# Block steps of a feed-forward layer spread over longer chains, with one weight sum on GpSimd

## The chip, the cores and the metric

The kernel runs on one core of a Trainium2 chip. The metric is the device time of one execution, in microseconds (us); the kernel before was timed three times. All times of single instructions below come from one profiled execution.

The engines go by short names: PE is TensorE's matmul, PEld its weight load, DVE VectorE, ACT ScalarE, POOL GpSimd, SP SyncE, which here only issues transfers. POOL and ACT issue transfers too. Each engine takes its instructions in order, and waits on semaphores for the others.

## The reference, cut to what matters

One layer of an encoder on 512 tokens of width 1024: a gated linear attention branch (GLA) and a forgetting attention branch (FoX), merged by gates and an output projection, and then the feed-forward part, which the change is about:

```python
def causal_dwconv(u, w, bias):
    S = u.shape[1]
    up = jnp.pad(u, ((0, 0), (CONV_W - 1, 0), (0, 0)))
    out = bias
    for j in range(CONV_W):
        out = out + w[j] * up[:, j:j + S]
    return out
...
    y = jax.nn.sigmoid(g_gla + gate_b[0]) * (o_gla @ w_gla_branch) \
        + jax.nn.sigmoid(g_fox + gate_b[1]) * (o_fox @ w_fox_branch)
    x = x + y @ w_out

    a, val = jnp.split(rmsnorm(x, norm_ffn_g) @ w_up, 2, axis=-1)
    a = causal_dwconv(a, conv_w, conv_b)
    return x + (jax.nn.gelu(a) * val) @ w_down
```

Everything is float32. `w_up` is 1024 x 5632, `w_down` 2816 x 1024; a last RMSNorm follows.

## The kernel before, in words

**Products.** Each float32 operand is split into two parts, high and low, of a format that TensorE takes in one pass; `mm3` makes one product of three matmuls (high x high, high x low, low x high: lines 200 to 202). An activation operand is split once. A weight comes in pieces of 128 x 1024 (512 KB): `load_raw` (L136) issues its transfer from SP into a tile `raw` or `rawx`, two of each, and `split_next` (L162) makes `wh` with a ScalarE copy (L180) and `wl` with a VectorE subtraction (L181). Three `wh`/`wl` pairs go round. `piece()` (L191) hands out pieces in the order of the list `recipes` and splits three ahead.

**Stages in order of time.** To about 130 us the GLA stage (first projections, the chunked recurrence); to about 250 us attention; to about 320 us the branch projections and gates; to about 380 us the output projection, in which each of eight tiles also adds into the sum of squares for the next norm; then two plain feature tiles of `w_up`, the up stage from about 404 us, the down stage from about 620 us, and the end.

**The up stage.** The product with `w_up` is done in blocks, seven products instead of eight for each 2 x 2 block product (Winograd's variant of Strassen's scheme). The remaining 20 feature tiles form ten groups `g`, each with seven *steps* p1 to p7. A step is 24 matmuls of 256 columns (`up_product`, L998). Its weight operand is a piece or a running sum of pieces: p5 needs u12 + u11, p6 adds u22 to p5's, p4 adds u21 to p6's, p7 adds u12 to p3's. Before, every such addition is a transfer that adds into the tile in SBUF, issued from GpSimd's queue (L149 for p5, L184 for the others). An add can only be issued once the piece before it has been split, and the next piece only be split once the add has landed. So p5-p6-p4 and p3-p7 are *chains*, and the order of the steps sets how much time each link has. `SLOT` (L55) gives each step a place in a cycle of seven; the steps of all groups are sorted by it.

The results meet in PSUM: p1 and p2 in a bank `x`, p5 and p3 in `z`, p6, p7 and p4 in `y`. After p1 and after p5 the bank is copied to SBUF (`joint`, L1027, ScalarE). After p6 VectorE adds p1's copy to `y` into a new tile (L1030), ScalarE writes that back over `y` in PSUM (L1031), and VectorE makes the first half of the convolution's input `ap` from it and `z` (L925 within `minus_sum`). After p7 comes the second half, the convolution and gelu (L966, L970, L975); after p4 the activations (L1046) and their block sums. The tile framework plans the order of each engine's queue from the program order and its own estimates, so instructions of neighbouring steps mix.

**Ahead of the up stage.** `rms_of_sum` (L287) makes the norm's factor: matmuls with ones (L291), a short VectorE chain, a matmul that broadcasts (L296), a copy into `rb`. Products of the first plain tile stand before and between. VectorE then scales all of `xs` (L928) and, with ScalarE, makes the seven activation operands (`split_x`, L920).

**The down stage** has the same seven products, with operands made of activations and weights; the four weight blocks that are sums (`wsum`) are made in DRAM by eight transfers of 2816 KB, four copies and four adds, each issued from GpSimd (L189) behind the split of the piece named in `SUM_AT` (L57), after a tiny copy `tick` (L187) that waits for that split. Pieces of the down stage are loaded four ahead, into `raw` and `rawx`. The product `p` = 0 uses a11, which is complete after half of the up stage's groups.

Of the kernel before, what the change touches and what calls it, by code (L numbers as in the profile page):

```python
# [54 lines left out]
SLOT = {1: -3, 5: -1, 2: 1, 3: 2, 6: 3, 7: 5, 4: 7}  # L55

SUM_AT = (24, 27, 30, 33, 38, 42, 46, 50)  # L57
# [7 lines left out]
def hybrid_kernel(ctx: ExitStack, tc, xT, wp, wu, wd, wf, pp, aw2, qkg, fing, out):  # L65
# [24 lines left out]
    def pax():  # L90
        return bank("ax")
# [19 lines left out]
    recipes = [((wf[n],), None, WF, None) for n in range(KD)] + [((w,), None, 1024, "raw") for w in wp_pieces(wp)]  # L111
    steps = sorted((7 * g + at, g, p) for g in range(NSS) for p, at in SLOT.items())
    steps = [(g, p) for _, g, p in steps]
    at_step = {}
    for g, p in steps:
# [7 lines left out]
    ND = len(recipes)  # L123
    for b in down_blocks:
        for i in range(NPB):
            m = min(1024, KB * 512 - i * 1024)
            place = "rawx" if (len(recipes) - ND) % (NRAW + NRAWX) >= NRAW else "raw"
            recipes.append(((b[:, i * 1024 : i * 1024 + m],), None, m, place))
    NP = len(recipes)
    follows = {r[1]: n for n, r in enumerate(recipes) if r[1] is not None}  # L130
# [5 lines left out]
    def load_raw(n):  # L136
        new, before, m, place = recipes[n]
        if before is not None:
            raws[n] = raws[before]
            return  # L140
        if n < KD:
            raws[n] = slabs[n]
        elif place == "raw":
            raws[n] = wpool.tile([P, 1024], F32, tag="raw", name="raw", bufs=NRAW)
        else:
            raws[n] = rawx_pool[0].tile([P, 1024], F32, tag="rawx", name="rawx", bufs=NRAWX)
        nc.sync.dma_start(raws[n][:, :m], new[0])
        for w in new[1:]:
            nc.gpsimd.dma_start(raws[n][:, :m], w, accum_op=ALU.add)  # L149

    def load_ahead(n):

        for i in range(n, min(NP, n + 6)):
            new, before, _, place = recipes[i]
            if place == "rawx":
                ahead = 6 if rawx_pool and i < ND else NRAW + NRAWX if rawx_pool else 0
            else:
# [1127 lines left out]
```

## Time and profile before

| | us |
|---|---|
| median of 3 runs (lowest, highest) | 740.61 (738.9, 741.93) |
| the profiled execution | 743.6 |
| its span, first to last instruction | 741.8 |
| PE busy | 714.4 (96%) |
| DVE busy | 518.7 (70%) |
| ACT busy | 407.4 (55%) |
| POOL busy | 166.9 (23%) |

In the rows of the profile `out<-in` names tiles; the two numbers of a timeline row are its start and its length in us; what stands in square brackets is idle time of that engine ahead of the instruction and what ended it. In a row of waits stand the engine and line that waited, what it waited for, and total us, times and longest. A window's row gives, for a stretch of time, its length, busy time and number of instructions of PE, PEld, DVE, ACT and POOL, the granted clock of TensorE, the busy share of the transfer engines and GB/s. A row of transfers ends with KB each and the median us from issue to landing. Matmuls are pipelined, so PE's busy share is not its share of the peak.

### The profile page before, as it was taken

To read this page: it belongs to the slowest core of one execution; us is meant where nothing else is said; L and a number is where in the kernel's file an instruction comes from. 1 tells how busy PE (TensorE), PEld (TensorE's weight loads), DVE (VectorE), ACT (ScalarE), POOL (GpSimd) and SP (SyncE) were. 2 spreads that over 40 slices of the span, in tenths; PEclk is the share of its full clock that TensorE was granted. 3 is DMA by queue.
4 is the path that set the end of the run, shared out by engine and by line. 5 is a ranking of instruction groups with operands and counts; after the bars stand their busy time and mean duration, and the time that the engine had idled before them with its cause. 6 is when DMAs were issued, how large, how long until landed. Compare 5 with 4: busy or idle time off the path is not lost.

```text
span 741.8 us, 11096 instructions
## 1 busy us (share of the span) xinstructions
PE 714.4 (96%) x4186; PEld 620.2 (84%) x4186; DVE 518.7 (70%) x787; ACT 407.4 (55%) x648; POOL 166.9 (23%) x190
## 2 busy tenths in 40 slices
PE   8999999999999999999999889899899998999996
PEld 6887788887888788877778789899899997888875
DVE  7875588577766654455439988577678876987876
ACT  7483333688778533225535556555455654655654
POOL 7133235224410321122320211011111101000113
PEclk9999999999999999999999999999999999999999
DMA  8052211787691987994564588788887888566653
GB/s 304 30 173 101 84 63 63 285 235 222 191 250 70 239 210 197 233 232 155 175 184 106 107 213 196 197 207 190 199 192 187 203 193 289 159 211 193 190 173 128
DMA packets 44117, 134.05 MB, mean 181 GB/s; under 512 B 4488, under 2 KB 11800, under 8 KB 43936
## 3 DMA queue, kind: packets, MB, share of 16 engines
q1 hardware_dynamic: 27552, 81.38, 33.8%
q0 software_dynamic: 10272, 46.66, 29.9%
q10 hardware_dynamic: 6240, 5.31, 2.2%
q8 instruction: 33, 0.54, 0.3%
q14 instruction: 20, 0.16, 0.1%
HBM read 129.12 MB, written 27.28 MB: 211 GB/s over the span
## 4 chain that ended last, share of the span: by engine, by line
PE 61%; DMA 17%; DVE 9%; issue 6%; ACT 4%; POOL 1%; SPq 0%; ACTq 0%; POOLq 0%; DVEq 0%
PE ps_mm L200 15%; PE ps_mm L201 14%; PE ps_mm L202 14%; DMA rawx<-in_wu_dram 7%; DMA raw<-in_wu_dram 6%; DVE wl L181 4%; PE ps_ax L201 4%; PE ps_ax L200 4%; PE ps_ax L202 4%; ACT wh L180 3%; DMA raw<-in_wp_dram 2%; DVE t L970 1%; DMA cb<-nct 1%; DMA rawx<-wsum 1%; PE ps_pt L737 1%
## 5 line engine op out<-in xcount | busy, mean ns | idle before, releaser
L180 ACT CAST wh<-raw 128x1024 fp32r<-128x1024 f32 x116 | 120.4, 1040 | 198.6 <-PE ps_mm L201 50.3
L181 DVE TENSOR_TENSOR wl<-raw,wh 128x1024 fp32r<-128x1024 f32 x116 | 153.2, 1323 | 74.8 <-ACT wh L180 73.8
L200 PE MATMUL ps_mm<-xh,wh 128*128 128x512 f32 (+1 forms) x288 | 102.0, 355 | 4.1 <-ACT ps_mm L1031 3.3
L202 PE MATMUL ps_mm<-xh,wl 128*128 128x512 f32 (+1 forms) x288 | 100.8, 351 | 0.0
L201 PE MATMUL ps_mm<-xl,wh 128*128 128x512 f32 (+1 forms) x288 | 100.8, 351 | 0.0
L200 PEld LDWEIGHTS ps_mm<-xh,wh 128*128 128x128 f32 x288 | 55.8, 194 | 11.4 <-ACT ps_mm L1031 4.1
L181 DVE TENSOR_TENSOR wl<-rawx,wh 128x1024 fp32r<-128x1024 f32 (+1 forms) x48 | 57.8, 1208 | 7.3 <-ACT wh L180 7.0
L202 PEld LDWEIGHTS ps_mm<-xh,wl 128*128 128x128 f32 x288 | 55.8, 194 | 7.4 <-DVE wl L177 0.4
L201 PEld LDWEIGHTS ps_mm<-xl,wh 128*128 128x128 f32 x288 | 56.0, 194 | 5.9
L180 ACT CAST wh<-rawx 128x1024 fp32r<-128x1024 f32 (+1 forms) x48 | 49.1, 1023 | 16.5 <-DMA rawx<-in_wu_dram 9.1
L200 PE MATMUL ps_mm<-wh,xh 128*128 128x512 f32 x140 | 55.4, 397 | 0.0
L201 PE MATMUL ps_mm<-wl,xh 128*128 128x512 f32 x140 | 54.7, 390 | 0.0
L202 PE MATMUL ps_mm<-wh,xl 128*128 128x512 f32 x140 | 54.6, 390 | 0.0
L184 POOL DMA_DIRECT2D rawx<-in_wu_dram x20 | 17.6, 879 | 112.1 <-DVE wl L181 110.3
L200 PE MATMUL ps_ax<-xh,wh 128*128 128x256 f32 x120 | 35.8, 299 | 5.1 <-ACT ps_ax L1031 5.1
L200 PE MATMUL ps_ax<-xo,wh 128*128 128x256 f32 x120 | 34.2, 285 | 3.1 <-ACT wh L180 3.1
L1113 POOL TENSOR_TENSOR xo<-xo 128x512 f32<-128x512 f32 (+1 forms) x9 | 12.2, 1362 | 106.2 <-ACT t L1104 102.7
L202 PE MATMUL ps_ax<-xh,wl 128*128 128x256 f32 x120 | 35.4, 297 | 0.1
L201 PE MATMUL ps_ax<-xl,wh 128*128 128x256 f32 x120 | 35.2, 293 | 0.0
L463 POOL TENSOR_TENSOR cb<-cb,negm 128x128 f32<-128x128 f32 x32 | 18.8, 597 | 70.2 <-DMA cb<-nct 57.6
L201 PE MATMUL ps_ax<-xo,wh 128*128 128x256 f32 x120 | 34.1, 284 | 0.0
L202 PE MATMUL ps_ax<-xo,wl 128*128 128x256 f32 x120 | 34.0, 283 | 0.0
(377 smaller groups left out, 1986.6 us busy)
## 6 DMA issues: line engine op xcount, KB each, us to landing
raw<-in_wp_dram SPq DMA_DIRECT2D x56, 512.0 KB, 4.1
wsum<-in_wd_dram POOLq DMA_DIRECT2D x6, 2816.0 KB, 18.4
raw<-in_wu_dram SPq DMA_DIRECT2D x30, 512.0 KB, 4.5
rawx<-in_wu_dram POOLq DMA_DIRECT2D x30, 512.0 KB, 5.8
wsum<-wsum POOLq DMA_DIRECT2D x2, 2816.0 KB, 21.6
raw<-wsum SPq DMA_DIRECT2D x11, 512.0 KB, 3.8
rawx<-in_wu_dram SPq DMA_DIRECT2D x10, 512.0 KB, 5.7
raw<-in_wu_dram POOLq DMA_DIRECT2D x10, 512.0 KB, 7.2
```

The source lines that it names most:

```text
L180: nc.scalar.copy(out=hi[:, :m], in_=raw[:, :m])
L181: nc.vector.tensor_sub(out=lo[:, :m], in0=raw[:, :m], in1=hi[:, :m].bitcast(F32))
L184: nc.gpsimd.dma_start(raw, recipes[follows[n]][0][0], accum_op=ALU.add)
L200: mm(ps, lhsT=ah, rhs=bh, start=start, stop=False, **k)
L201: mm(ps, lhsT=ah, rhs=bl, start=False, stop=False, **k)
L202: mm(ps, lhsT=al, rhs=bh, start=False, stop=stop, **k)
L463: nc.gpsimd.tensor_add(out=cb[:, o + n - P : o + n], in0=cb[:, o + n - P : o + n], in1=negm)
L737: nc.tensor.transpose(pt[:, c], pr[:, c], ident)
L970: nc.vector.scalar_tensor_tensor(out=t0[:, i], in0=ap[:, i, w : w + T], scalar=col(C_CW + w * NF + f), in1=t0[:, i], op0=ALU.mult, op1=ALU ...
L1113: nc.gpsimd.tensor_mul(out=x3, in0=x3, in1=fgt[:, c])
```

## The change

- *Longer chains.* New `SLOT`: p3 and p7 of a group, and p6 and p4, stand six steps apart (before 3 and 4); p5 and p6 stay four apart; p5 and p3 have one other step between them (before two). In the first group p6 comes one step later than its slot.
- *Buffers and loads.* The p3-p7 chain has two tiles `rawy` of its own, p5-p6-p4 the two `rawx`, p1 and p2 the two `raw`. What to do after a piece has been split (issue the add for a later step, load a later piece, make the first sum) is written out in a table `then`. The first loads of p5 and p3 of two groups are issued as soon as the pool for the up stage opens.
- *One weight sum by GpSimd.* p5's u12 + u11 is now a 128 x 1024 addition on GpSimd of two loaded pieces (u11 is p1's), queued behind the add issued after p6's split of the group before.
- *p1 joined in PSUM.* VectorE adds p1's copy to `y` in place in PSUM, and the write back by ScalarE goes. p3's bank is copied to SBUF too, `ap`'s first half is made from that copy, and `z` and `y` always use the banks `mm`, `x` the banks `ax`.
- *Ahead of the up stage.* Four and three k-steps of the plain tile stand before and between the norm's matmuls (before 2 and 4). `xs` is scaled in four blocks of 128 x 1024, in the order in which the operands p1, p5, p3 need them; the first plain `ap` product comes right after p1's operand.
- *End of the up stage.* The first two pieces of down product 0 stand behind p2 and p7 of the last group, and the pieces of the down stage are loaded six ahead, into all six raw tiles. a21's successor `s1` is split over the four pieces of product 0 that remain.
- *Sums of the last weights.* `SUM_AT` moves from pieces 24 to 50 to pieces 12 to 41. Pieces 12, 16 and 20 belong to the GLA stage.
- The scratch for the descriptors of GpSimd's transfers is set to 8192 bytes, and `ap` loses 48 columns.

```diff
-SLOT = {1: -3, 5: -1, 2: 1, 3: 2, 6: 3, 7: 5, 4: 7}
+SLOT = {1: -1, 5: 0, 3: 2, 6: 4, 2: 5, 7: 8, 4: 10}
+EARLY = (2, 7)
-SUM_AT = (24, 27, 30, 33, 38, 42, 46, 50)
+SUM_AT = (12, 16, 20, 24, 28, 32, 36, 41)
...
+    steps = sorted((7 * g + at + 1.5 * (g == 0 and p == 6), g, p) for g in range(NSS) for p, at in SLOT.items())
...
-            1: ((u11,), None, "raw"), 2: ((u21,), None, "raw"), 3: ((u22,), None, "raw"), 5: ((u12, u11), None, "rawx"),
-            6: ((u22,), 5, "rawx"), 4: ((u21,), 6, "rawx"), 7: ((u12,), 3, "raw"),
+            1: (u11, None, "raw"), 2: (u21, None, "raw"), 3: (u22, None, "rawy"), 7: (u12, 3, "rawy"),
+            5: (u12, None, "rawx"), 6: (u22, 5, "rawx"), 4: (u21, 6, "rawx"),
...
+    for g in range(NSS):
+        for p, q in ((5, 6), (3, 7), (6, 4)):
+            behind(at_step[g, p], "add", at_step[g, q])
+        if g + 1 < NSS:
+            behind(at_step[g, 6], "first sum", at_step[g + 1, 5], at_step[g + 1, 1])
+            behind(at_step[g, 1], "load", at_step[g + 1, 1])
+            behind(at_step[g, 2], "load", at_step[g + 1, 2])
+        if g + 2 < NSS:
+            behind(at_step[g, 7], "load", at_step[g + 2, 3])
+            behind(at_step[g, 4], "load", at_step[g + 2, 5])
+    behind(NPLAIN - 2, "load", at_step[0, 1])
+    behind(NPLAIN - 2, "first sum", at_step[0, 5], at_step[0, 1])
+    behind(NPLAIN - 1, "load", at_step[0, 2])
+
+    freed = [at_step[NSS - g, p] for g, p in ((1, 1), (2, 7), (2, 4), (1, 2), (1, 7), (1, 4))] + at_last
+    for n, i in zip(freed, at_last):
+        behind(n, "load", i)
...
+    def first_sum(n, other):
+        nc.gpsimd.tensor_add(out=raws[n], in0=raws[n], in1=raws[other])
...
-    plain_products(plain[0], up, range(2))
-    rms_of_sum(ssum, rt, rb, cpool, "r1", between=lambda: plain_products(plain[0], up, range(2, 6)))
-    plain_products(plain[0], up, range(6, KD))
+    plain_products(plain[0], up, range(4))
+    rms_of_sum(ssum, rt, rb, cpool, "r1", between=lambda: plain_products(plain[0], up, range(4, 7)))
+    plain_products(plain[0], up, range(7, KD))
...
-    for k in range(KD):
-        nc.vector.tensor_mul(out=xs[:, k], in0=xs[:, k], in1=rb)
+    scale_x(x11, 0)
     split_x(1, x11)
-    nc.vector.tensor_sub(out=x3, in0=x11, in1=x21)
-    nc.vector.tensor_sub(out=x21, in0=x22, in1=x21)
-    split_x(5, x21)
+    nc.vector.tensor_mul(out=ap[:, 0, 2 : T + 2], in0=plain[0][0], in1=rb)
+    scale_x(x21, 1)
+    scale_x(x22, 1)
+    nc.vector.tensor_sub(out=x3, in0=x22, in1=x21)
+    split_x(5, x3)
     plain.append((pmm(), pmm()))
     up = (piece(), piece())
     plain_products(plain[1], up, range(KD))
+    nc.vector.tensor_sub(out=x21, in0=x11, in1=x21)
+    minus_sum(x11, x3, x11)
+    scale_x(x12, 0)
+    minus_sum(x3, x12, x11)
+    split_x(3, x3)
     split_x(2, x12)
-    minus_sum(x11, x21, x11)
-    minus_sum(x12, x12, x11)
-    split_x(3, x12)
     split_x(6, x11)
-    split_x(7, x3)
+    split_x(7, x21)
     split_x(4, x22)
...
-        if p == 1 or p == 5:
-            st[p] = joint()
-            nc.scalar.copy(out=st[p], in_=ps)
+        if p in (1, 5, 3):
+            st[p] = joint(ps)
         elif p == 6:
-            u = joint()
-            nc.vector.tensor_add(out=u, in0=ps, in1=st[1])
-            nc.scalar.copy(out=ps, in_=u)
-            minus_sum(ap[:, :, 2 : H + 2], halves(st["z"]), halves(u))
+            nc.vector.tensor_add(out=ps, in0=ps, in1=st[1])
+            minus_sum(ap[:, :, 2 : H + 2], halves(ps), halves(st[3]))
...
+        if g == NSS - 1 and p in EARLY:
+            first_down(EARLY.index(p))
...
-    acc1 = [pax(), pax()]
-    product(0, acc1)
+    left = range(len(EARLY), NPB)
+    for i in left:
+        first_down(i)
+        w = -(-KB // len(left))
+        split_act(1, operands[1], slice((i - left[0]) * w, min((i - left[0] + 1) * w, KB)))
...
-    nc = bacc.Bacc("TRN2", target_bir_lowering=False, num_devices=1)
+    nc = bacc.Bacc("TRN2", target_bir_lowering=False, num_devices=1, dynamic_dma_scratch_size=8192)
```

More of the change, by code (lines that the diff above doesn't have):

```diff
@@ L122, in hybrid_kernel, with behind @@
         recipes.append((new, at_step[g, before] if before else None, 1024, place))
[L123 to L130, printed above, removed]
+        if g == NSS - 1 and p in EARLY:
+            at_last.append(len(recipes))
+            recipes.append(last_pieces[len(at_last) - 1])
+    for r in last_pieces[len(at_last) :]:
+        at_last.append(len(recipes))
+        recipes.append(r)
+    then = {}
+    def behind(n, *what):
+        then.setdefault(n, []).append(what)
+    for g in range(NSS):
[14 more added lines that the diff above has]
+        behind(n, "load", i)
     raws, splits, taken, first_copy = {}, [], [0], []
@@ L136, in load_raw @@
     def load_raw(n):
[L137 to L140, printed above, removed]
+        new, _, m, place = recipes[n]
         if n < KD:
@@ L888, in hybrid_kernel @@
     rawx_pool.append(npool)
+    for g in range(2):
+        for p in (5, 3):
+            load_raw(at_step[g, p])
     plain = []
```

91 lines of the change are left out of this document (55 added, 36 removed).

## The prediction

> **What bounds the kernel now.** I read the page first, then the waits of TensorE, the windows with its granted clock, the chain of waits where TensorE stood, the transfers, and last VectorE's timeline ahead of the up stage.
>
> ```profile
> span 741.8 us, 11096 instructions
> ...
> PE 61%; DMA 17%; DVE 9%; issue 6%; ACT 4%; POOL 1%; SPq 0%; ACTq 0%; POOLq 0%; DVEq 0%
> ```
>
> TensorE carries 61% of the chain, transfers 17%. The change takes no matmul away, so only TensorE's idle time can be gained. Its waits (total, times, longest, us):
>
> ```profile
> PE ps_ax L200 <- ACT wh L180: 5.6, 2, 3.1
> PE ps_ax L200 <- ACT ps_ax L1031: 5.1, 4, 2.0
> PE ps_mm L200 <- ACT ps_mm L1031: 3.3, 3, 2.1
> ...
> PE ps_ax L201 <- DVE wl L181: 0.9, 1, 0.9
> PE ps_mm L201 <- DVE yl L855: 0.8, 1, 0.8
> ...
> PE ps_mm L200 <- ACT yh L853: 0.7, 1, 0.7
> PE ps_ax L291 <- POOL ap L962: 0.7, 1, 0.7
> ```
>
> The long ones lie in or around the up stage, in which one step of 24 matmuls takes 2.9 us (the first and the 25th start):
>
> ```profile
> 404.18 0.28 PE L200 MATMUL ps_ax<-xo,wh 128*128 128x256 f32 x1
> ...
> 407.05 0.28 PE L200 MATMUL ps_ax<-xo,wh 128*128 128x256 f32 x1
> ...
> 598.97 0.28 PE L202 MATMUL ps_mm<-xo,wl 128*128 128x256 f32 x1
> 600.06 0.39 PE L200 MATMUL ps_ax<-xh,wh 128*128 128x256 f32 x1 [0.81 <-ACT ps_ax L1031]
> ```
>
> The last two rows show that a wait costs more than its listed idle time: 1.09 us from start to start instead of 0.12, so 0.97 for a listed 0.81, or 0.16 more. And a long one is paid twice, in the granted clock (the column 0.50; first and last of the five half-speed windows, and a clean stretch):
>
> ```profile
> 335.90:339.20 3.30, 3.30 (x11) 2.57 (x11) 2.93 (x3) 2.18 (x4) 1.04 (x1) 0.50 0.22 88
> ...
> 622.60:625.90 3.30, 3.30 (x18) 3.30 (x17) 0.12 (x1) 0.00 (x0) 0.00 (x0) 0.50 0.97 410
> 475.80:533.50 57.70, 57.70 (x483) 57.70 (x482) 41.72 (x55) 33.01 (x42) 9.48 (x11) 1.00 0.87 201
> ```
>
> At half speed 18 matmuls fit in 3.3 us; at the clean stretch's rate (483 in 57.7) it would be 27.6. Ten lost ones are 1.2 us, half of the window would be 1.65; I take 1.5 for each. The five lie at 336, 414, 472, 537 and 623 us, each behind a wait of TensorE. [...]
>
> What ended last at a stall of the middle (the chain of waits):
>
> ```profile
> 459.12 8.78 DMA raw<-in_wu_dram
> ...
> 468.00 1.06 ACT wh L180
> ...
> 469.08 1.23 DVE wl L181
> 470.31 0.61 DVE joint L1030
> ...
> 470.94 0.60 ACT ps_ax L1031
> ```
>
> ```profile
> ACT wh L180 <- DMA raw<-in_wu_dram: 38.2, 9, 6.1
> ```
>
> A weight added onto another by transfer (p7 behind p3) landed late, ScalarE and VectorE waited for it in order, and p6's join, which does not need that weight, was queued behind: TensorE waited for the join's write back into PSUM. ScalarE's nine such waits (row above) add up to 38.2 us.
>
> **The change, part by part.** The transfers' prices (KB each, median us to landing):
>
> ```profile
> raw<-in_wp_dram SPq DMA_DIRECT2D x56, 512.0 KB, 4.1
> ...
> rawx<-in_wu_dram POOLq DMA_DIRECT2D x30, 512.0 KB, 5.8
> wsum<-wsum POOLq DMA_DIRECT2D x2, 2816.0 KB, 21.6
> ...
> rawx<-in_wu_dram SPq DMA_DIRECT2D x10, 512.0 KB, 5.7
> raw<-in_wu_dram POOLq DMA_DIRECT2D x10, 512.0 KB, 7.2
> ```
>
> *1. Longer chains, own buffers.* A step's weight is split two steps ahead at the earliest, since three wh/wl pairs go round; the split ends about 0.9 step later (1.06 + 1.23 us above). From p3 to p7 there were 3 steps (8.6 us) for an add of 7.2 (8.8 at the stall) plus a split of 2.3: too short. Now p3-p7 and p6-p4 are 6 steps apart (17.3 us) and p5-p6 stays 4 (11.5). With an add of even 8.8 us and a split of 2.3 the six-step chains keep 6.2 us; the four-step one keeps 3.4 at the usual 5.8, as it did before. Forty accumulating transfers become 30, in buffers of their own per chain, so that each load on SP waits only for the split just ahead of it. I take all L1031 waits of the middle as gone: 5.1 + 3.3 less the 0.8 at the end of the stage = 7.6 us, with two half-clock windows 3.0: **10.6 us**.
>
> *2. p1 joined in PSUM by VectorE.* The add of about 0.6 us stays, the 0.6 us copy back by ScalarE goes, and one ScalarE copy for p3 comes. Counts are equal, TensorE's wait after p6 is 0.6 shorter, and p7 follows four steps later instead of two. No gain beyond item 1.
>
> *3. The weight sum by GpSimd.* Ten 128x1024 additions replace ten 512 KB adding transfers. Nearest rows, GpSimd and VectorE in the GLA stage:
>
> ```profile
> 53.45 2.62 POOL L483 TENSOR_TENSOR e<-kg,e 128x1024 f32<-128x1024 f32 x1 [1.87 <-ACT e L474]
> ...
> 58.66 2.60 DVE L181 TENSOR_TENSOR wl<-raw,wh 128x1024 fp32r<-128x1024 f32 x1 [1.51 <-ACT wh L180]
> 62.88 1.22 DVE L181 TENSOR_TENSOR wl<-raw,wh 128x1024 fp32r<-128x1024 f32 x1 [1.61 <-ACT wh L180]
> ```
>
> So 2.6 us instead of 5.8, and up to 1.4 us more for the VectorE instruction beside it. VectorE is idle 16.0 of 57.7 us in the clean stretch, 5.6 per group of seven steps, so 1.4 fits. [...] The new tight place is this sum. Counted from the start of p5 of group g+1: p5 of g+2 is loaded once p4 of g is split, which may begin after one step (2.9) and is done by 5.5 to 7; plus 5.7 of load and 2.6 of sum it is there at 13.8 to 15.3, and with 2.3 of split at 16.1 to 17.6, for a step that begins at 20.2. GpSimd stands waiting for that load, with nothing queued behind but the add after the same p5. If the cover of 2.6 us goes, each lost us is paid ten times.
>
> *4. Start of the up stage.* Four instead of two k-steps ahead of the norm's matmuls hide the 0.7 us wait on L291. But VectorE is the bound there:
>
> ```profile
> 391.30:413.40 22.10, 19.03 (x108) 16.42 (x106) 22.10 (x25) 13.28 (x15) 0.86 (x1) 1.00 0.44 97
> ```
>
> It is busy for all 22.1 us from rb to the third step's wl, while TensorE waits 3.1. The change has four scales of 128x1024 for eight of 128x512, and the same seven splits, four sums, three wl and two ap products. Seven k-steps of six matmuls stand ahead of rb's instead of six: 1.4 us more (266 matmuls in 60 us, the window shown under item 5), less the stall's 0.86, so rb comes 0.5 us later. So I give back the 0.7 and take a **loss of 0.5**, with the 3.1 and its clock window left. Ends: -4.6 (the third step's operands come ahead of p6's, p7's and p4's) to +3 (two convolution instructions, 1.5 us, now ready early, push in ahead, and a further window).
>
> *5. End of the stage.* Two pieces of the first down product fill the gaps around p7 and p4 of the last group, and their weights load early, each behind an up weight.
>
> ```profile
> 620.13 0.73 PE L200 MATMUL ps_ax<-wh,acth 128*128 128x512 f32 x2 [2.54 <-ACT wh L180]
> 621.66 0.38 PE L200 MATMUL ps_mm<-xh,wh 128*128 128x256 f32 x1 [0.80 <-ACT ps_mm L1031]
> ...
> 640.00:700.00 60.00, 60.00 (x266) 49.51 (x265) 50.62 (x64) 36.10 (x53) 3.52 (x2) 1.00 0.63 190
> ```
>
> 2.5 + 0.8 + one window 1.5 = 4.8 us. Only four pieces of product 0, 42 matmuls or 9.5 us, are left to cover the splitting of s1, and VectorE is busy 50.6 of 60 us in that stage; I give back 0.5. The load of x2d waits for xo, which p1, p5 and p3 now leave earlier; it falls beside the last adds, which have five steps to land, and costs nothing unless these are late. **4.3 us**.
>
> *6. Sums of the last weights moved.* The last sum collided with the load that the output projection needed:
>
> ```profile
> 314.22 1.01 POOL L189 DMA_DIRECT2D wsum<-wsum  x1 [3.08 <-DMA wsum<-wsum]
> ...
> 320.25 11.35 DMA raw<-in_wp_dram
> ...
> 334.01 0.61 DVE yl L855
> ```
>
> 11.35 us for a 4.1 us load. Without it the 0.7 and 0.8 us waits and the window at 336 go: **3.0 us**. The sums are now issued behind pieces 12 to 41, three of them in the GLA stage. Each slows one or two loads from about 4 to 11 us, by 7. Pieces there are split early (VectorE, then ScalarE, which takes the freed buffer):
>
> ```profile
> 108.72 1.23 DVE L181 TENSOR_TENSOR wl<-raw,wh 128x1024 fp32r<-128x1024 f32 x1 [0.27 <-ACT wh L180]
> ...
> 119.17 1.05 ACT L180 CAST wh<-raw 128x1024 fp32r<-128x1024 f32 x1 [3.75 <-PE ps_mm L202]
> ```
>
> The piece split at 108.7 is first used when the product before it ends, at 119.2: 9 us, which cover the 7. Not covered are ScalarE's copies queued behind a late split, and L483, ahead of which the tick copy and the issue (1.01 us above) now stand on GpSimd. I take a **loss of 1.0** (ends 0 and 5: one load too late and a clock window).
>
> *7. Six raw buffers down the last stage* instead of four: the wait of 0.9 on the last weights goes, **0.9 us**:
>
> ```profile
> 713.45 5.96 DMA rawx<-wsum
> ```
>
> The descriptor scratch cut in half costs nothing that the trace can show: GpSimd's issue above took 1.01 us, and its wait was for another transfer's landing. Ends: 0 and 1 us in all; I take 0, since no row shows a full ring.
>
> **Sum.** 10.6 + 4.3 + 3.0 + 0.9 = 18.8, and 0.16 for each of 11 waits that go, 1.8: 20.6. Less 0.5 (start) and 1.0 (moved sums): **19.1 us**. The profiled execution took 743.6 us (span 741.8), 3.0 above the median of 740.61; it becomes 724.5, and the median **721.5**.
>
> **Rivals.**
> A. *A new wait in each group; the change ends slower.* p3 now follows p5 in the same PSUM bank with one step between, where two stood, and ScalarE must have copied p5 out in those 2.9 us. If its queue holds the copy behind a late weight, TensorE waits as in the L1031 rows: 2.0 + 0.16 + 1.5, 3.7 us in each of ten groups, 37 us: 721.5 + 37 = 758. It decides from six groups on (22 us). Against it: p7 and p4 had one step between them all along, with longer work in it, and the clean stretch of 57.7 us has no wait there. Chance 0.04.
> B. *p5's sum comes late* because load and GpSimd need 3 us more than above: 1 us in each group, 10 us: 731. Chance 0.12.
> C. [...] Chance 0.05.
> D. *The stalls come from the order of the queues and not from late transfers*: then they move and stay: 740. Against it the chain above, whose 8.78 us no order explains. Chance 0.05.
> E. *The moved sums hurt* the GLA and attention stages: 5 us more: 726. Chance 0.13.
> F. *The start clears too*: 3.1 + 1.5 + 0.2 less: 716.5. Chance 0.14.
>
> **How the numbers follow.** The forecast has 0.47, and 721.5 is its time. Its own range is 718 to 725 (item 6 from 0 to 2.5, item 5 and 4 by 1.5 each way). The range to 0.8 takes in F's best end with item 6 at no cost (712) and B with item 6's bad end, short of C (734); A, D and half of C lie outside. Half a per cent (3.7 us) is about what a measurement of this kernel can tell from none. Faster: forecast, F, E, B, C, 0.91, less 0.04 for an unseen trouble of that size: 0.87. Same: D and a little, 0.06. Slower: A and a little, 0.07.
>
> **What would show it.** The L1031 rows are gone from TensorE's waits with nothing in their place above 1 us in all; ScalarE's wait for raw<-in_wu_dram (38.2 us) falls under 10; the half-clock windows fall from five to one, at the start of the up stage; the 11 us load near 320 is about 4; from the first up step to the first of product 1 some 16 us less. Wrong it would be if TensorE waits for joint copies or for wl of p5 in each group, if GpSimd's sum takes over 4 us, or if the GLA stage ends later by more than 3 us.

## The result, and the profile after

| | before | after |
|---|---|---|
| median of 4 runs (lowest, highest), us | 741.12 (738.9, 741.93) | 736.68 (735.85, 737.21) |
| profiled execution (span), us | 743.6 (741.8) | 736.88 (735.2) |
| ratio, 95% interval | | 0.9944 [0.9919, 0.9968] |

The change makes the kernel faster by 0.6%, 4.4 us where 19.1 were forecast; 736.7 lies above the range (712 to 734). Between the two profiled executions the difference is 6.7 us, and all stretches below are of these two. Medians, here and below, are of all executions, while the ratios leave out those more than 1.5% above the fastest of the same kernel, which takes away seven of twelve for "sums spread" below, because one of its executions took 731.6 us.

The page of the changed kernel, its span and its chain:

```profile
span 735.2 us, 11057 instructions
...
PE 72%; DVE 11%; DMA 10%; issue 3%; ACT 3%; POOL 1%; SPq 0%; DVEq 0%; ACTq 0%; POOLq 0%
```

Transfers fell from 17% to 10% of the chain, VectorE rose from 9% to 11%. The waits of TensorE (total, times, longest) and two of ScalarE; the last row is TensorE's in the kernel before:

```profile
PE ps_pt L768 <- ACT pr L759: 6.1, 4, 2.9
PE ps_mm L233 <- DVE wl L206: 3.0, 5, 0.9
PE ps_mm L231 <- DVE ap L1034: 1.9, 1, 1.9
PE ps_ax L233 <- DVE wl L206: 1.6, 2, 1.3
PE ps_mm L232 <- DVE xo L956: 1.3, 1, 1.3
```

```profile
ACT wh L205 <- DMA raw<-in_wp_dram: 29.4, 9, 7.7
ACT wh L205 <- DMA rawx<-in_wu_dram: 11.0, 4, 4.5
```

```profile
PE ps_pt L737 <- ACT pr L728: 0.7, 1, 0.7
```

The rows for L1031 are gone. ScalarE's waits for transfers of the up weights were 38.2 us for `raw` and 9.1 for `rawx`; the row of 11.0 is what stands there now, with 3.7 more for GpSimd's sum. But at the top stands a wait that was small before: TensorE, in the attention stage, for ScalarE's `pr` (0.7 us in all before). The others lie at the start of the up stage, but for some small ones for `wl` later on. Windows there and in the middle (length; busy time and count of PE, PEld, DVE, ACT, POOL; granted clock; transfers' share; GB/s):

```profile
415.40:425.66 10.26, 7.27 (x30) 6.71 (x31) 9.51 (x11) 4.66 (x7) 4.13 (x3) 0.50 0.37 75
425.70:548.50 122.80, 122.80 (x1025) 122.80 (x1025) 96.81 (x111) 70.38 (x89) 37.71 (x26) 1.00 0.79 182
```

In the second TensorE never stops for 122.8 us. The first is three half-clock windows in a row, where the kernel before had one.

To place the gains and losses I took, at the end of each stretch, the start of the matmul of the same number in both programs (each has 4186), after minus before. In the up stage the order of the steps differs, and so there the number of matmuls counts and not which ones they are. For example, the first of the up stage starts at 404.18 before and 404.90 after, the 100th at 421.47 and 427.82. What a stretch added to that difference:

| stretch (us, kernel before) | after minus before, us | forecast |
|---|---|---|
| GLA, to 183 | 0 | part of the loss of 1.0 |
| attention, 183 to 260 | +4.6 | rest of that loss |
| output projection, to 341 | -3.6 | -3.3 |
| norm, plain tiles, to 404 | -0.2 | +0.5 with the next row |
| start of the up stage (four steps), to 421 | +5.6 | |
| middle and end of the up stage, to 650 | -12.5 | -16.2 |
| down stage | -0.5 | -1.1 |
| sum | -6.6 | -19.1 |

The forecasts hold the 0.16 per wait where the wait was. Three rows fall short: the start of the up stage (5.4 lost with the row above it, 4.9 more than forecast), the middle (3.7 less gained) and attention (3.6 more lost).

**Attention.** The chain of waits ahead of TensorE's second long stall there, and ScalarE's timeline:

```profile
201.11 19.34 DMA raw<-in_wp_dram
...
220.53 1.04 ACT wh L205
221.57 0.41 ACT pr L759
```

```profile
216.12 0.19 ACT L752 ACTIVATION_READ_ACCUMULATOR pr<-ln,nm 128x1 f32 x1
220.53 1.04 ACT L205 CAST wh<-raw 128x1024 fp32r<-128x1024 f32 x1 [4.22 <-DMA raw<-in_wp_dram]
221.47 0.51 ACT L759 ACTIVATE pr<-pr,rs 128x256 f32<-128x256 f32 x1
```

A weight's 512 KB took 19.3 us: a sum of 2816 KB had been issued just ahead (195.0 to 218.0), and three loads of `cb` between. The weight is not needed yet. But its split stands in ScalarE's queue ahead of the softmax's `pr`, and so ScalarE stood still for 4.2 us and TensorE for 2.9. At 245 us the difference is 6.4; 1.9 of it comes back by 260, mostly where two waits of the kernel before are gone.

**Start of the up stage.** VectorE and GpSimd, and TensorE's two longest waits:

```profile
392.68 1.83 DVE L963 TENSOR_TENSOR xs<-xs,rb 128x1024 f32<-128x1024 f32 x1 [3.42 <-ACT rb L331]
...
405.33 3.35 DVE L206 TENSOR_TENSOR wl<-rawx,wh 128x1024 fp32r<-128x1024 f32 x1
...
418.47 1.21 DVE L206 TENSOR_TENSOR wl<-rawy,wh 128x1024 fp32r<-128x1024 f32 x1
```

```profile
391.04 2.39 POOL L179 TENSOR_TENSOR rawx<-rawx,raw 128x1024 f32<-128x1024 f32 x1
404.50 3.09 POOL L179 TENSOR_TENSOR rawx<-rawx,raw 128x1024 f32<-128x1024 f32 x1 [11.06 <-PE ps_mm L233]
```

```profile
415.54 0.58 PE L232 MATMUL ps_mm<-xo,wh 128*128 128x256 f32 x1 [1.35 <-DVE xo L956]
418.03 0.55 PE L231 MATMUL ps_mm<-xh,wh 128*128 128x256 f32 x1 [1.91 <-DVE ap L1034]
```

The same ends of VectorE's stretch in the kernel before, the first scale behind `rb` and the third step's `wl`:

```profile
391.28 2.50 DVE L928 TENSOR_TENSOR xs<-xs,rb 128x512 f32<-128x512 f32 x4 [4.74 <-ACT rb L300]
...
413.20 1.22 DVE L181 TENSOR_TENSOR wl<-raw,wh 128x1024 fp32r<-128x1024 f32 x1
```

VectorE is busy from 392.7 to 425 without a break. `rb` came 1.4 us later than before (392.68 against 391.28), but 0.95 of that was there at 380 us already, carried in from attention. From the start of that scale, right behind `rb`, to the end of the third step's `wl` it was 23.1 us (to 414.4) and is 27.0 (to 419.7). These 3.9 us are GpSimd's first two sums, which took 0.6 from the scale and 2.1 from the `wl` beside them, and two convolution instructions (0.66 each) that stand ahead. Part of TensorE's gaps from 411 to 420 is paid again, in the clock (0.50 from 415.4 to 425.66).

**Middle of the up stage.** Four waits of TensorE for `wl` between 548 and 618 us (2.7 us listed, 3.3 with the 0.16 of each). The chain ahead of the first, and GpSimd and VectorE there:

```profile
533.46 8.27 DMA rawx<-in_wu_dram
```

```profile
545.67 2.71 POOL L179 TENSOR_TENSOR rawx<-rawx,raw 128x1024 f32<-128x1024 f32 x1 [0.38 <-DMA rawx<-in_wu_dram]
```

```profile
544.05 4.88 DVE L1011 SCALAR_TENSOR_TENSOR t<-ap,ppt,t 128x512 f32<-128x512 f32 x4
```

An adding transfer took 8.27 us, where the median of these is 5.8. So a split came late on VectorE, and the four convolution instructions behind it fell beside GpSimd's sum and took 4.88 us instead of 2.74. The next step's `wl` stood behind them, and TensorE waited 1.3 us for it. The second run of experiment 12 has the same stall (1.33 us at 542.9, behind an add of 8.29); runs 1, 4 and 6 do not have it. What makes that add late in some executions no run isolates.

### The profile page after: what moved, and what is told of

The parts are those of the page before. It is cut to its first block, busy times and chain, and to the rows that moved or that the text cites. A ratio compares the mean times of both kernels' runs of the same rounds, so it can differ in the third digit from the quotient of the medians.

```text
span 735.2 us, 11057 instructions
## 1 busy us (share of the span) xinstructions
PE 710.0 (97%) x4186; PEld 616.5 (84%) x4186; DVE 531.0 (72%) x781; ACT 406.7 (55%) x646; POOL 188.2 (26%) x190
## 4 chain that ended last, share of the span: by engine, by line
PE 72%; DVE 11%; DMA 10%; issue 3%; ACT 3%; POOL 1%; SPq 0%; DVEq 0%; ACTq 0%; POOLq 0%
PE ps_mm L231 18%; PE ps_mm L233 18%; PE ps_mm L232 18%; DMA raw<-in_wp_dram 5%; PE ps_ax L233 4%; PE ps_ax L231 4%; PE ps_ax L232 4%; DVE wl L206 4%; DMA rawx<-in_wu_dram 4%; DVE t L1011 1%; ACT wh L205 1%; POOL rawx L179 1%; DMA cb<-nct 1%; PE ps_ax L909 1%; PE ps_ax L631 0%
## 5 line engine op out<-in xcount | busy, mean ns | idle before, releaser
L205 ACT CAST wh<-raw 128x1024 fp32r<-128x1024 f32 x89 | 93.0, 1047 | 114.7 <-PE ps_mm L232 51.9
L206 DVE TENSOR_TENSOR wl<-raw,wh 128x1024 fp32r<-128x1024 f32 x89 | 127.9, 1438 | 31.3 <-ACT wh L205 28.6
L233 PE MATMUL ps_mm<-xh,wl 128*128 128x512 f32 (+1 forms) x328 | 111.2, 339 | 1.0 <-DVE wl L206 1.0
L232 PE MATMUL ps_mm<-xl,wh 128*128 128x512 f32 (+1 forms) x328 | 110.9, 339 | 0.0
L205 ACT CAST wh<-rawy 128x1024 fp32r<-128x1024 f32 x33 | 34.6, 1048 | 31.7 <-PE ps_ax L232 26.1
L233 PE MATMUL ps_mm<-xo,wl 128*128 128x256 f32 x160 | 46.7, 292 | 1.9 <-DVE wl L206 1.9
L232 PE MATMUL ps_mm<-xo,wh 128*128 128x256 f32 x160 | 46.5, 291 | 1.3 <-DVE xo L956 1.3
L231 PE MATMUL ps_mm<-xo,wh 128*128 128x256 f32 x160 | 46.3, 289 | 0.9 <-ACT joint L1055 0.9
L206 DVE TENSOR_TENSOR wl<-rawy,wh 128x1024 fp32r<-128x1024 f32 x33 | 40.0, 1218 | 8.2 <-ACT wh L205 8.2
L231 PE MATMUL ps_mm<-xc,wh 128*128 128x256 f32 (+1 forms) x136 | 44.9, 330 | 0.0
L232 PE MATMUL ps_mm<-xc,wh 128*128 128x256 f32 (+1 forms) x136 | 44.6, 328 | 0.0
L233 PE MATMUL ps_mm<-xc,wl 128*128 128x256 f32 (+1 forms) x136 | 44.6, 328 | 0.0
```

Of the source, the lines that this page charges most:

```text
L205: nc.scalar.copy(out=hi[:, :m], in_=raw[:, :m])
L206: nc.vector.tensor_sub(out=lo[:, :m], in0=raw[:, :m], in1=hi[:, :m].bitcast(F32))
L231: mm(ps, lhsT=ah, rhs=bh, start=start, stop=False, **k)
L232: mm(ps, lhsT=ah, rhs=bl, start=False, stop=False, **k)
L233: mm(ps, lhsT=al, rhs=bh, start=False, stop=stop, **k)
```

## The experiments

The ratio is to the kernel before, run on the same chip (its median 741 to 742 in each group). "Both back" is the base of the later ones; lines there are 3 higher (`wl` is L209).

| run | median, us | ratio, 95% interval |
|---|---|---|
| the change | 736.7 | 0.9944 [0.9919, 0.9968] |
| sums back | 730.5 | 0.9871 [0.9828, 0.9914] |
| sums spread | 743.5 | 0.9956 [0.9905, 1.0007] |
| start by transfer | 731.9 | 0.9879 [0.9842, 0.9916] |
| p2 third | 738.6 | 0.9954 [0.9925, 0.9982] |
| both back | 726.5 | 0.9789 [0.9725, 0.9853] |
| both back, ap early | 728.4 | 0.9814 [0.9751, 0.9877] |
| both back, all ten sums by transfer | 743.1 | 1.0005 [0.9969, 1.0040] |
| old slots | 743.2 | 1.0008 [0.9971, 1.0046] |
| both back, two splits later | 727.9 | 0.9837 [0.9791, 0.9884] |
| that, p2 third, p6 later | 726.8 | 0.9829 [0.9782, 0.9876] |
| before with the new sums | 746.7 | 1.0075 [1.0041, 1.0110] |
| both back, nothing early | 728.8 | 0.9843 [0.9785, 0.9900] |
| two splits and plain tiles later | 725.7 | 0.9789 [0.9742, 0.9837] |
| later still | 725.0 | 0.9765 [0.9710, 0.9821] |
| both back, norm early | 726.7 | 0.9795 [0.9751, 0.9840] |

**1. The sums of the last weights back.**

```diff
-SUM_AT = (12, 16, 20, 24, 28, 32, 36, 41)
+SUM_AT = (24, 27, 30, 33, 38, 42, 46, 50)
```

> The changed kernel, with the sums of the last weights back at the pieces where they stood before (24 to 50). The changed kernel's median is 736.7 us. Theory 1: the 6.1 us in which TensorE waits for ScalarE's pr at L759 in the attention stage come from loads that land behind a 2816 KB sum (19.3 and 17.4 us for 512 KB), with ScalarE's queue standing behind the split of that load. Then these waits fall under 1.5 us, matched matmuls after attention are 4.7 us earlier, the loss at 332 to 340 us (3.4 us) is back: 736.7 - 4.7 + 3.4 = 735.4. Rival: the attention waits come from another part (order of the queues, the smaller descriptor scratch) and stay: 736.7 + 3.4 = 740.

Measured 730.5. TensorE's waits from 170 to 235 us:

```profile
PE ps_pt L768 <- ACT pr L759: 0.7, 1, 0.7
```

Matmuls after attention are 4.3 us earlier, as theory 1 said. The gain is larger than expected, since of the loss near 333 us only 1.3 came back, without a half-clock window, and of the four small waits for `wl` between 548 and 618 us (3.3 us in the change's execution) one of 0.3 is left; why the others are absent no run isolates. With the sums at the old places the output projection is still 2.4 us shorter than in the kernel before.

**2. The same in the kernel before.** Only `SUM_AT` is changed, to the new places.

> The kernel before, with nothing changed but the places of the sums of the last weights (pieces 12 to 41 instead of 24 to 50). Theory (the moved sums alone make the attention waits, by the loads behind them): TensorE's waits at L737 of the kernel before rise from 0.7 to about 6 us, matmuls after attention are 4 to 5 us later, and the losses at 332 to 340 us (3.4) go: 741.5 + 1 = 742.5. Rival (the attention waits need the new kernel's loads or descriptor scratch): no such waits, 741.5 - 3.4 = 738.

Measured 746.7 against 742.2. Its waits from 170 to 240 us, and two loads of the chain there:

```profile
PE ps_pt L737 <- ACT pr L728: 5.2, 3, 2.4
```

```profile
162.82 17.68 DMA raw<-in_wp_dram
...
203.51 18.74 DMA raw<-in_wp_dram
```

The same loads are as late without any other part of the change. With run 1 this settles it: the moved sums make the attention waits. It is 4.2 us more than the 742.5 forecast: the attention stage lost 6.7 us, with two half-clock windows (from 186.5 and 224.1), and the output projection gave back 3.6.

**3. The sums spread otherwise.** `SUM_AT = (16, 20, 24, 27, 30, 33, 38, 42)`.

> The changed kernel, with the sums behind pieces 16, 20, 24, 27, 30, 33, 38, 42: two in the GLA stage, where the changed kernel lost nothing, those of the attention stage where they stood before, the last one near 267 us. Theory 1 (a sum costs what the next load is late by, so the place decides and not the number): the attention waits go and the loss at 332 to 340 us stays away: 736.7 - 4.7 = 732.0. Rival (any two sums more ahead of 250 us take their 4 to 5 us somewhere in GLA or attention): 736 to 737.

The forecast failed: 11 of 12 executions took 739.6 to 746.8 us, one 731.6. The chain of waits, and ScalarE's timeline:

```profile
213.16 19.47 DMA raw<-in_wp_dram
...
232.71 1.05 ACT wh L205
```

```profile
232.71 1.04 ACT L205 CAST wh<-raw 128x1024 fp32r<-128x1024 f32 x1 [6.41 <-DMA raw<-in_wp_dram]
233.66 0.58 ACT L775 CAST ph<-ps_pt 128x512 fp32r<-128x512 f32 x1
```

The sum behind piece 33 starts at 203.4 us in run 1 and at 210.2 here. In both, three `cb` loads and a weight are issued behind it, but here within 3 us and there within 5.4. The weight lands 19.5 us after issue (14.1 in run 1), and TensorE stops for 5.2 us. This fits theory 1, by which the place among the transfers decides; but a piece number does not fix that place, and the forecast of 732 was wrong. That the number of sums plays no part is not shown.

**4. The first two weight sums by transfer.**

```diff
     def first_sum(n, other):
+        if n in (at_step[0, 5], at_step[1, 5]):
+            nc.gpsimd.dma_start(raws[n], recipes[other][0], accum_op=ALU.add)
+            return
         nc.gpsimd.tensor_add(out=raws[n], in0=raws[n], in1=raws[other])
```

> The changed kernel, with the first two of GpSimd's ten weight sums (those at 391 and 404.5 us) made by an adding transfer. Theory 2a, sharing: VectorE's wl beside the second sum takes 1.2 instead of 3.35 us and its scale beside the first 1.2 instead of 1.83; VectorE is busy without a break there, so the wl that the third step waits for comes 2.7 us earlier and one of three half-clock windows (1.5 us) goes: 736.7 - 4.2 = 732.5. Rival 2b, order: the third step is p3, whose operand stands behind five VectorE instructions that p2's did not need, and plain ap products stand behind all splits; the shared time only fills a wait: within 1 us, 736.

Measured 731.9, 4.8 us less (2a said 4.2). VectorE:

```profile
393.69 1.23 DVE L966 TENSOR_TENSOR xs<-xs,rb 128x1024 f32<-128x1024 f32 x1 [3.42 <-ACT rb L334]
...
405.73 1.23 DVE L209 TENSOR_TENSOR wl<-rawx,wh 128x1024 fp32r<-128x1024 f32 x1
```

1.23 instead of 1.83, and 1.23 instead of 3.35. One of three half-clock windows went. That is 2a's mechanism, but the nearness of the number is luck: in the profiled executions the start of the up stage gives 2.5 us, that window included (and 2.5 again between runs 1 and 6). Another 2.9 lie between 530 and 615 us, where the small waits of the changed kernel are missing as in run 1, and 1.4 from there to 644, which no run isolates.

**5. p2 as third step.** In the first group p2's slot is 3.5 earlier, and its operand is made ahead of p3's.

> The changed kernel, with p2 of the first group as third step again and its operand made ahead of p3's. Theory 2b, order: p2's operand needs one scale and one subtraction where p3's needs five instructions (5.7 us), and the wait of TensorE for p5's copy out of PSUM (0.9 us) gets a step between: the waits from 411 to 420 us fall from 8 to about 4 us and two of three half-clock windows (3 us) go: 736.7 - 6 = 731. Rival: VectorE's whole amount between rb and the last operand is the bound and the stall only moves to the fourth or fifth step: within 1.5 us of 736.7.

Measured 738.6. Theory 2b failed: the stall moved to the fourth step, p3, and grew. TensorE, and ScalarE's queue ahead of it:

```profile
418.74 0.58 PE L231 MATMUL ps_mm<-xh,wh 128*128 128x256 f32 x1 [5.57 <-ACT joint L1055]
```

```profile
416.21 1.04 ACT L205 CAST wh<-rawx 128x1024 fp32r<-128x1024 f32 x1 [2.88 <-DMA rawx<-in_wu_dram]
...
418.11 0.58 ACT L1055 COPY joint<-ps_mm 128x512 f32<-128x512 f32 x1
```

p5's copy out of PSUM stands behind p6's weight, which is still being added by transfer.

**6. Both back** (runs 1 and 4 together).

> Both at once: the sums of the last weights back at pieces 24 to 50, and the first two weight sums of the up stage by transfer. Measured so far: 736.7 us for the changed kernel, 730.5 with the first alone (6.2 less), 731.9 with the second alone (4.8 less). Theory (two separate losses, one in the attention stage, one at the start of the up stage): they add up, 736.7 - 6.2 - 4.8 = 725.7. Rival (part of each gain is that later transfers and sums fall otherwise against each other, common to both, as the small waits at 548 to 618 us that went in both kernels): 728 to 729.

726.5: the two losses add up in the medians (10.2 us of 11.0). In the profiled executions it is 11.3 of 6.8 + 6.4, since the small waits near 548 to 618 us are missing in both parts and count once. TensorE has no wait in the output projection, though the sums are back, and that stage is 3.3 us shorter than in the kernel before. The middle, from 417.6 us on, is clean:

```profile
417.60:630.00 212.40, 212.35 (x1694) 208.61 (x1693) 178.63 (x211) 126.67 (x161) 52.07 (x39) 1.00 0.79 196
```

**7. All ten first sums by transfer.** `first_sum` is always the `dma_start` of run 4.

> As the kernel with both back, and all ten first sums of the up stage by adding transfers, none by GpSimd. Theory A (the sum's 3.4 us on GpSimd, and what it takes from VectorE, is absorbed in the middle, and the 5.8 us transfer would bring the weight at 19.3 to 20.8 us for a step that begins at 20.2): waits of 0.5 us or so for that weight in some of eight groups with a half-clock window or two, 4 us more: 730. Theory B (six-step chains have enough room, GpSimd's sum brings nothing): no wait, VectorE's wl at 1.22 us, within 1 us of the kernel with both back.

743.1, 16.5 us more. Theory A was right in kind and four times too small:

```profile
PE ps_mm L233 <- DVE wl L206: 5.0, 7, 0.9
PE ps_mm L231 <- ACT wh L205: 4.3, 4, 2.2
```

p5's weight came late in six groups (one add, issued at 460.9 us, took 8.5), with three half-clock windows in the middle. GpSimd's sum carries the middle, although it costs at the start.

**8. The old order of steps** in the changed kernel (`SLOT` of before).

> The changed kernel with the order of steps from before (SLOT 1: -3, 5: -1, 2: 1, 3: 2, 6: 3, 7: 5, 4: 7), its own buffers, loads, GpSimd sum and PSUM join kept. Theory (the longer chains carry the gain of 15.5 us that the stretch from 426 to 643 us shows): p7's and p4's weights come late in most groups, TensorE waits about 10 us in all with four or five half-clock windows: 736.7 + 12 = 749. Rival (buffers of their own and loads in a written-out order carry it, and the join without ScalarE): waits under 2 us in the middle, 736 to 739, since the start may move by 2 us with p2 as the third step.

743.2, 6.5 us more, between the two forecasts. The waits and the chain at one of them:

```profile
PE ps_mm L231 <- DVE ap L959: 4.8, 8, 1.2
```

```profile
467.68 5.51 DMA rawy<-in_wu_dram
...
473.29 1.06 ACT wh L205
...
474.37 1.23 DVE wl L206
475.59 0.62 DVE ps_mm L1096
```

It is the stall of the kernel before, in eight groups: p7's weight is late, and p6's join stands behind its split on VectorE. Of 205.2 us from 424.8 on TensorE is idle 6.9, each wait is 1.2 us or less, and no window goes to half clock. So the order of steps is worth 4.9 us of the 12.5 from 421 to 650 us in the profiled executions, and 6.5 in the medians; the rest lies in the other parts together.

**9. The second ap product early** (right behind the second plain tile's matmuls).

> As the kernel with both back, and the second plain tile's ap product placed in program order right behind that tile's matmuls, ahead of five operand sums. TensorE waited 2.1 us for that product (L1037 there), because its PSUM bank is the one that p6's result goes to. Theory: the wait goes, later operands come 0.6 us later, and of two half-clock windows one goes: 725.7 - 1.5 - 1.5 = 722.7. Rival (the bound is VectorE's whole amount, the wait moves to the next weight or operand): within 1 us of the kernel with both back.

728.4, no gain. One wait took the place of three:

```profile
415.76 0.58 PE L236 MATMUL ps_mm<-xo,wl 128*128 128x256 f32 x1 [4.53 <-DVE wl L209]
```

**10. Splits of p7's and p4's operands behind p5.**

```diff
-    split_x(7, x21)
-    split_x(4, x22)
...
         up_product(ps, p, first)
+        if (g, p) == (0, 5):
+            split_x(7, x21)
+            split_x(4, x22)
```

> As the kernel with both back (726.5 us), and the operands of p7 and p4, which are needed five and more steps later, are split behind step p5 of the first group in program order instead of ahead of the first step. Theory (VectorE's amount of work ahead of the third step's wl is the bound): two subtractions of 1.14 us fewer stand ahead of it, TensorE's waits from 407 to 414 us fall by 2.3 and one of two half-clock windows (1.5) goes: 722.7. Rival (the order of PSUM banks and ScalarE's copies is the bound, as the run with the early ap product suggests, where one wait only took the place of three): within 1 us of 726.5.

727.9, 1.4 us above both back: the rival is nearer. In the profiled execution (725.5) the waits from 407 to 411 fell (2.1 + 1.0 + 0.9 + 0.9 became 1.0 + 0.6 + 0.6 + 0.9) with one half-clock window fewer, and small ones came later (0.8 at 418, 0.9 at 631). There the theory's mechanism shows; in the medians its gain does not.

**11. That with p2 third and p6 behind p1 of the second group.**

> As the kernel with the two splits deferred, with p2 third in the first group again, and p6 of the first group placed behind p1 of the second, so that no weight that comes by an adding transfer stands ahead of p5's copy in ScalarE's queue (that cost 5.6 us in the run with p2 third). Theory: p5's copy has a step of 2.9 us, its wait (0.9) goes, and p3's operand and weight have a step more: waits at the start fall below 2 us and no half-clock window is left: 726.5 - 4 - 3 = 719.5. Rival: VectorE still comes to the third step's wl at the same time, and the waits stay as with the deferred splits alone: 722 to 726.

726.8: the wait for p5's copy is gone, but TensorE waits 2.9 us for p2's `wl` and three times more for 0.8 to 0.9, with two half-clock windows. The theory's 719.5 was wrong.

**12. The plain tiles' convolutions behind p3 and, in a second run, behind p2.** Both with the two splits deferred, in the second behind p3; the second `ap` product stays ahead of the steps.

> As the kernel with two splits deferred (727.9, profiled 725.5), with the plain tiles' convolution and products behind step p3 of the first group in program order, and only the second ap product ahead. Theory (VectorE's amount ahead of the third step's wl is the bound): two convolution instructions of 0.66 us fewer stand there; TensorE's waits from 406 to 412 us (0.9 + 0.6 + 1.0 + 0.6 listed) fall by 1.3 and the last half-clock window (1.5) goes: 2 to 3 us less, 725. Rival (the order of banks and copies): the wait moves to p6's or p1's operands or to the plain tiles' banks, within 1 us of 727.9.

> As the run before in this call, with everything put off by one more step (convolutions behind p2, the two splits behind p3). The place ahead of the third step's wl has the same work, so by the theory of VectorE's amount the first waits are the same as there, and later weights come 1 to 2 us earlier: 0 to 1 us less, 724.5. Rival: p4's and p7's operands or the plain tiles' banks now come late, 2 us more.

725.7 and 725.0. TensorE at the start, first run:

```profile
409.98 0.39 PE L234 MATMUL ps_mm<-xo,wh 128*128 128x256 f32 x1 [0.90 <-ACT joint L1057]
411.42 0.39 PE L234 MATMUL ps_mm<-xh,wh 128*128 128x256 f32 x1 [1.06 <-ACT wh L208]
```

Up to 427 us none of the waits for VectorE is left; what ends last now is ScalarE (p5's copy, then p6's weight). That is what the theory of VectorE's amount asks for; in the second run's profiled execution the start of the up stage takes 1.4 us less than in the kernel before. But one half-clock window (412.3 to 415.7) stays in both, which the forecast had gone. The first median is 2.2 us below that with the splits alone; the intervals overlap, so in the times the gain is likely and not shown.

**13. The norm's matmuls as before** (behind two plain k-steps, four between).

> As the kernel with both back (726.5), with the norm's matmuls placed as before: two plain k-steps ahead, four between. Theory (VectorE is the bound from rb on): rb comes 1.4 us earlier, the waits at 407 to 414 us shrink by as much and perhaps one of two half-clock windows (1.5) goes, and TensorE's 0.7 us wait at the norm's first matmul (1.0 from start to start) comes back: 726.5 - 1.4 + 1 = 726.1 without the window, 724.6 with it. Rival (the waits do not hang on rb): 727.5.

726.7, no change against both back. `rb` comes earlier, and the time goes into a wait for ScalarE's `wh` (2.2 us, p6's weight) and the old 0.7 at the norm.

**14. Nothing of the down product early** (`EARLY = ()`).

> As the kernel with both back (726.5 us), without the two pieces of the first down product between the last steps (EARLY empty); six buffers and the loads ahead stay. Theory (the two pieces fill waits of 2.5 and 0.8 us and a half-clock window): about 4 us more, 730.5. Rival (these waits came from late weights, which longer chains and six buffers cure by themselves): within 1 us, 726 to 727.5.

728.8 (724.7 to 731.3) against 726.5 (725.6 to 727.7): unclear in the times. In the profile TensorE has no wait at the end of the stage above 0.6 us, where the kernel before had 2.5 and 0.8. So the early pieces are not needed against them; which of the longer chains, the six buffers and the loads ahead cures them was not run.

## Why the prediction was wrong

**Right.** *Items 1, 2, 3 and 5 together* (the up stage past its start): 12.5 us of 16.2. In runs 1, 4 and 6, which lack the small waits near 548 to 618 us or nearly so, this stretch is 15.6, 16.8 and 17.0 us shorter than before, so the size was right and the waits are what is missing. The order of steps (run 8) and GpSimd's sum (run 7) both carry it. The text had priced item 3 as a hidden operation; without it 16.5 us go, so that it is a condition of item 1's gain. Item 5's gain came, but not through the pieces to which I gave it (run 14). Of what was to be seen, the L1031 rows went, though with 2.7 us of waits for `wl` in the middle and not under 1; the load near 320 us that took 11 takes 3.1; ScalarE's wait fell to 11.0 (under 10 was asked); GpSimd's sum stayed under 4 us (2.4 to 3.9, median 3.4, not 2.6). The half-clock windows are three and all at the start, not one; from the first up step to product 1 it is 6.8 us less, not 16.

**Luck: item 6, the gain, 3.3 forecast, 3.6 measured.** The collision with the last sum is real in the kernel before, where moving the sums alone brings 3.6 (run 2). But in the changed kernel with the sums at their old places the output projection is still 2.4 us shorter than before (run 1) and 3.3 with both back (run 6). So there the move brings 1.3 or less, for a loss of 4.6 in attention; what else shortened that stage no run isolates.

**Wrong: item 4, the start of the up stage, 0.5 forecast, 5.4 measured (5.6 less 0.2).** The step that failed is item 3's sentence "so 1.4 fits". I read VectorE's idle time in the middle and held it against all ten sums. But two of the ten run at 391 and 404.5 us, in the stretch of which item 4 said that VectorE is busy for all of it. There what GpSimd takes from VectorE is paid: 2.7 us of VectorE's time, 2.5 of TensorE's in run 4. The rival at 735 (C, chance 0.05: VectorE late by 1.4 us beside each of GpSimd's ten sums, 14 us, just above the range's end of 734) had the mechanism, spread over ten groups where it mostly does not bind (once, at 545 us, for 1.3 us), and not in the one place where it does. No run shows TensorE losing 1.4 us in each of ten groups; lost were the 2.5 at the first two sums and those 1.3. The size was off too: 2.1 us for a `wl`, not 1.4. In the trace the `wl` that takes 1.21 alone took 3.35 beside the sum and ended 1.1 us behind it (408.68 against 407.59); without the sum, in run 4, it took 1.23. The rest of the loss is VectorE's amount of work, which I counted as unchanged without asking what stands ahead of the third step: the third step is p3 and no longer p2, and two convolution instructions came in between (1.3 us), which item 4 had named as its bad end. `rb` was not the cause: without what it carried in from attention it came 0.5 us later, as forecast. Moving one piece of the work moves the wait (runs 5, 9, 13); putting off several brings most waits away (run 12). The ends given, -4.6 to +3, were too narrow, since they left the two sums out and had one further half-clock window where two came.

**Wrong: item 6, the loss, 1.0 forecast, 4.6 measured.** It is rival E (3.6 us more than forecast where E had 5), in attention alone; GLA lost nothing. Two numbers failed. The moved sum was to slow a load "from about 4 to 11 us"; beside the `cb` loads of attention it is 17 to 19. And the cover of 9 us was read from a GLA row and used for attention, where the split stands in ScalarE's queue ahead of the softmax. "Not covered are ScalarE's copies queued behind a late split" was the right sentence, turned round: it is what stands behind the split that pays.

*Item 7*: the wait at 713 is gone, 1.3 us where 1.1 was forecast, but 0.7 was lost again between 650 and 700 us. *Rivals*: A did not come in the groups; run 5 shows it in one place, at 5.6 us. B did not come: p5's weight is late only when a transfer makes its sum. D is refuted by the clean middle. F is refuted: the start grew. *The range*: its low end, 712, does not come out of its terms; F's 716.5 with item 6 at no cost is 715.5.

A version with both back and with more of VectorE's work put off beats both kernels: 725.0, ratio 0.9765 [0.9710, 0.9821]. That is 3.5 us above the forecast. Its lead over both back (726.5) is within the noise.

## What to carry to other kernels

Where an operation recurs, find the instance that falls into the tightest stretch and price it there; idle time of an engine elsewhere does not cover it. For a transfer that is moved, ask which loads fall behind it, and then what stands *behind the consumer* of such a load in its engine's queue, for that is who waits, even if the load itself is early. A stall that is cured by one instruction's place has likely only moved, as in runs 5, 9 and 13: undo or put off the whole amount of work before saying what bounds.

## What the runs showed of the hardware

A 128x1024 subtraction on VectorE that began 0.8 us behind a 128x1024 addition on GpSimd took 3.35 us where such a subtraction alone takes 1.21: 2.14 more, with 2.26 of the addition left when it began. I had taken the 2.60 of the profile before for the price.

The five half-clock windows of the kernel before lasted 3.41 us each, the three in a row of the changed kernel 10.24 together, and two in run 6 from 410.7 to 417.5; the wait alone does not tell whether one comes. The changed kernel's four waits in attention, the longest of 2.9 us, cost none; in run 5, whose attention stage is the same, a wait of 2.4 us cost one (from 185.4), and in run 2 waits of 2.4 and 2.1 us cost one each; the 5.2 us of run 3 cost three; eight of 0.3 to 1.2 us, spread over as many groups, cost none in run 8. The windows of the changed kernel around its longest, and of run 3:

```profile
218.80:230.00 11.20, 7.49 (x41) 5.85 (x40) 6.06 (x16) 7.70 (x18) 3.60 (x7) 1.00 0.38 142
```

```profile
231.90:242.00 10.10, 6.92 (x21) 5.75 (x22) 3.94 (x10) 5.07 (x11) 1.11 (x2) 0.50 0.34 116
```

A flat 1.5 us for each wait near 2 us, as in the prediction, is therefore only an average: 2.9 us in the changed kernel's attention brought no window, and the start of its up stage, where the longest wait is 1.9 us, three. What sets the clock no run isolates.

In the kernel before, each of the 24 matmuls of the up stage's first step, on split operands, shows as one record, 0.12 us apart and 0.28 long; the four matmuls of the norm at L291, on plain float32 operands, show as eight.
